# Weight sums between DRAM and DRAM, and a convolution tap added by an accumulating DMA, in a two-layer encoder kernel

## The chip, the core and the metric

The kernel runs on one core of a Trainium2 chip. The core has five engines that run side by side, each through its own queue of instructions: TensorE (PE: matrix products, with PEld loading its stationary operand), VectorE (DVE), ScalarE (ACT), GpSimd (POOL) and SyncE (SP, which here only issues transfers). Sixteen DMA engines move data for all of them. Tiles live in SBUF (128 partitions), products are collected in PSUM banks of 128 x 512 words. The metric is the device time of one execution in microseconds, the median of several; less is better.

## What is computed

Two layers, each a mixer of four branches followed by a convolutional FFN, over 512 tokens of 1024 channels, all in float32. The change touches the FFN's two later parts; of the mixer it matters that RMSNorm and the rotation of queries and keys come early in it. Cut to that:

```python
def _depthwise_conv(u, w, b):            # per channel, width 3, in the FFN
    y = lax.conv_general_dilated(u, w[:, None, :].astype(u.dtype), (1,), [(p, p)], ...)
    return y + b.astype(u.dtype)

def _conv_ffn(h, w_up, conv_w, conv_b, w_down):
    u = _depthwise_conv(h @ w_up, conv_w, conv_b)
    gate, up = jnp.split(u, 2, axis=-1)
    return (jax.nn.silu(gate) * up) @ w_down

def reference(...):
    for l in range(DEPTH):
        h = _rmsnorm(x, g_mix[l])
        proj = h @ w_in[l]
        ...
        cq = _partial_rope(_rmsnorm(cq, dil_qn[l]), cos, sin)
        ...
        x = x + mixed @ w_out[l]
        x = x + _conv_ffn(_rmsnorm(x, g_ffn[l]), w_up[l], ffn_conv_w[l], ffn_conv_b[l], w_down[l])
    return x
```

D_FF is 2816, so the FFN has 44 channel tiles of 128 (22 gates and 22 ups), and the down-projection contracts over 22 tiles, taken as 11 pairs.

## The kernel before

Every float32 product is three matmuls in a faster format: a weight is split into a high and a low part (`w_hi` by ACT, L222; `w_lo` by DVE, L224), an activation likewise, and high x high, low x high and high x low are summed in PSUM (`prod`, L243 to L245). Weights come in units of 128 x 1024 words, loaded by SP (L218) into `w_raw`. `unit` keeps two units ahead (`LOOK`), and three buffers hold splits. So a weight on its way to TensorE passes SP, ACT and DVE, in this order.

**Start of a layer.** `start_norm` and `norm_tile` make the scaled input and the sum of its squares. `finish_norm` turns that into 1/rms (`rstd`), which is needed along the tokens as a row for all partitions. It gets there through DRAM: POOL writes `row<-rstd` (L358) and reads it back as a broadcast, `raw<-row` (L362); ACT reorders it into `RB` (L366), which scales the products that leave PSUM. ACT's RB stands in front of the next `w_hi` splits. Then come the projections. For the dilated and the windowed branch, POOL rotates the first 16 channels of each head of Q in place (`qk_stats`, L510 to L513), and DVE scales Q after that (L519).

**Side work.** Attention, convolution and norms are generators in a list `side`. `tick` advances each by one step between blocks of TensorE's work, under `issue_after(self.last_mm.ins)`, which ties the instructions of a step that are TensorE's own behind the last matmul. What other engines get from a step is put in order by the scheduler: on each engine it takes what is ready by its own estimate of times, older work first.

**FFN** (`ffn`). A round i makes a gate tile and an up tile. Each is a block of 24 matmuls in one bank; DVE scales it into `U` (L915, with a zero column at either end); ACT writes the middle tap and the bias into `cy` (L918), and DVE adds the left and the right tap (L919, L920). ACT takes SiLU of the gate (`fth`, L924), DVE multiplies (`fl`, L931).

**Down-projection** (`down`). The contraction is a Winograd form of the product of 2 x 2 blocks, with seven products in place of eight. It needs sums of activations (`split_pair`, DVE) and sums of weights. A pair j of 128-row tiles has four weight quarters of 512 columns, b11, b12, b21 and b22; `weight_sums(l, j)`, called in every second round of the FFN, loads them into SBUF by POOL (`load_quad`, L971), forms t3, b12, t2 and b21 by four DVE subtractions (L978 to L981), and POOL stores the four to DRAM (L984). `last_units` lists the weight units of the down-projection, quarters from W and sums from that store; `w_raw<-sums` on SP reads them.

Of the kernel before, what the change touches and what calls it, by code (L numbers as in the profile page):

```python
# [31 lines left out]
NP2 = NF // 2  # L32

# [155 lines left out]
class Trunk:  # L189
# [484 lines left out]

    def attention(self, kind, V, yi):
# [214 lines left out]
    def ffn(self, l, last):  # L890
# [9 lines left out]
        self.load_quad(l, 0)  # L900
        for i in range(NF):
# [5 lines left out]
            if i % 2 == 0:  # L907

                with self.tc.issue_after(self.last_mm.ins):
                    self.weight_sums(l, i // 2)  # L910
            for s in range(2):
                c = i + s * NF
                ps = pss[s]
                u = U[(2 * i + s) % 4]
                v.tensor_tensor(u[:, 1:513], ps, self.RB, ALU.mult)  # L915
                y = self.fp.tile([P, S], F32, name=f"cy{s}", tag=f"cy{s}", bufs=2)
                w = lambda t: self.par('ffn_conv_w', c * 3 + t)
                nc.scalar.activation(y, u[:, 1:513], AF.Identity, scale=w(1), bias=self.par('ffn_conv_b', c))  # L918
                v.scalar_tensor_tensor(y, u[:, 0:512], w(0), y, ALU.mult, ALU.add)  # L919
# [35 lines left out]
    def last_units(self, l):  # L955

        quad = lambda j, q: self.quads[l][j][:, q * S:(q + 1) * S]
        sums = lambda j, a, b: self.sums[l][j][:, a * S:b * S]
        units = []
        for j in range(NP2):  # L960
            units.append(lambda j=j: [quad(j, 0), sums(j, 0, 1)])
            units.append(lambda j=j: [sums(j, 1, 3)])
        for f in (lambda j: quad(j, 2), lambda j: sums(j, 3, 4), lambda j: quad(j, 3)):
# [3 lines left out]
    def load_quad(self, l, j):  # L967

        self.quad = [self.fp.tile([P, 1024], F32, name="quad", tag="w_more", bufs=2) for _ in range(2)]
        for q in range(2):  # L970
            self.nc.gpsimd.dma_start(self.quad[q], self.quads[l][j][:, q * 1024:(q + 1) * 1024])  # L971

    def weight_sums(self, l, j):

        v = self.nc.vector
        (b11, b12), (b21, b22) = ((t[:, :S], t[:, S:]) for t in self.quad)
        t3, t2 = (self.fp.tile([P, S], F32, name=n, tag=n, bufs=1) for n in ("t3", "t2"))
        self.after_mm(v.tensor_tensor(t3, b22, b12, ALU.subtract))  # L978
# [3 lines left out]
        self.sums[l][j] = self.dram.tile([P, 4 * S], F32, name=f"sums{j}", tag=f"sums{j}", bufs=1)  # L982
        for n, t in enumerate((t2, b12, t3, b21)):
            self.nc.gpsimd.dma_start(self.sums[l][j][:, n * S:(n + 1) * S], t)  # L984
        if j + 1 < NP2:
            self.load_quad(l, j + 1)

    def pair_tags(self, j):
# [9 lines left out]
        s4 = (late[6:8], late[8:10], ["e6", "e7"], x[12:14], x[14:16], ["t3", "t2"])[j // 2]  # L998
        return hi + lo + a + s4

    def conv_tile(self, tag):
        w = {'U': 514, 'c': S}[tag[0]] + 4 * PHASE * (tag == 'U3')
        return self.fp.tile([P, w], F32, name=tag, tag=tag, bufs=1 if tag[0] == 'U' else 2)

    def split_pair(self, F, j, got):
# [5 lines left out]
        def tile(t):  # L1011
            pool = self.xpool if t[:2] in ("xh", "xl") else self.fp
            return pool.tile([P, S], F32R, name=f"p{t}", tag=t, bufs=2 if t in ("lo", "xr", "xn", "cy0", "cy1") else 1)
# [9 lines left out]
        def split(h, l, x):  # L1023
# [3 lines left out]
        v.tensor_tensor(a[:, lo], fi[:, hi], fk[:, hi], ALU.add)  # L1027
# [5 lines left out]
        v.tensor_tensor(fk[:, lo], fk[:, lo], a[:, hi], ALU.subtract)  # L1033
        split(bh, bl, fk[:, lo])
        cut = lambda h, l, c: [(h[:, c + b * P:c + (b + 1) * P], l[:, c + b * P:c + (b + 1) * P]) for b in range(2)]
        got[j] = {'a11': cut(ih, il, 0), 's3': cut(ih, il, 256), 'a12': cut(kh, kl, 0), 'a22': cut(kh, kl, 256),
                  's1': cut(ah, al, 0), 's2': cut(ah, al, 256), 's4': cut(bh, bl, 0)}

    def down(self, F, last):
# [24 lines left out]
        if last:  # L1064
            for b, h in ((2, 1), (3, 1), (0, 1), (1, 1), (2, 0), (3, 0), (0, 0), (1, 0)):
                nc.sync.dma_start(xt[b, h], self.resT[b * P:(b + 1) * P, h * S:(h + 1) * S])
            u = [self.fp.tile([P, S], F32, name="xn", tag="xn", bufs=2) for _ in range(2)]
        else:
            u = [xt[0, 1], xt[1, 1]]
# [8 lines left out]
        for b in range(2):  # L1078
            add(u[b], B[b])
        for b in range(2):  # L1080
            if last:
                add(xt[2 + b, 1], C[b])
            else:
                v.tensor_tensor(xt[2 + b, 1], u[b], C[b], ALU.add)
            add(xt[2 + b, 1], E[b])
        if last:
            for b in range(2):
                for t in (xt[2 + b, 1], xt[2 + b, 0], xt[b, 1]):
                    add(t, u[b])
                self.store(xt, 2 + b, 1)  # L1090
        for banks, x, n, h in ((A, 'a12', 0, 0), (E, 'a22', 2, 0), (C, 's4', 0, 1)):
# [11 lines left out]
            for b in range(2):  # L1103
# [7 lines left out]
                elif banks is E:  # L1111
                    v.tensor_tensor(t, u[b], banks[b], ALU.add)
# [26 lines left out]
    def run(self):  # L1139
        nc, tc = self.nc, self.tc  # L1140
        with ExitStack() as st:
# [8 lines left out]
            self.quads, self.sums = [], []  # L1150
            for l in range(L):
# [9 lines left out]
                self.sums.append([None] * NP2)  # L1161
# [48 lines left out]
    def layer(self, l):  # L1210
# [3 lines left out]
        with tc.tile_pool(name="gate", bufs=1, reuse_waits="tile") as self.gp:  # L1214
            with tc.tile_pool(name="attn", bufs=1, reuse_waits="tile") as self.ap:
# [5 lines left out]
                with self.first():  # L1221
                    for _ in self.qk_stats(Q, 4, 4, None):
# [5 lines left out]
                                 self.attention('na', V, 1)))  # L1228
                Vd = self.new_V()
# [37 lines left out]
        with tc.tile_pool(name="ffn", bufs=1, reuse_waits="tile") as self.fp:  # L1267
            self.scratch = lambda: self.fp.tile([P, S], F32, name="raw", tag="cy0", bufs=2)
# [59 lines left out]
```

## Time and profile before

| | |
|---|---|
| Median of 3 runs | 1559.25 us (1559.11 to 1559.95) |
| Span of the profiled execution, first to last instruction | 1556.7 us (the page gives no other time of it) |
| Mean granted clock of TensorE | 0.999 |
| First U of the FFN (L915) in layer 0, last `fl` (L931) in layer 1 | 452.42 us, 1456.30 us |
| First and last product of the down-projection | 673.01 us, 1552.05 us |
| DMA, whole span | 244.86 MB, 157 GB/s |

The profile is one execution, traced by the hardware. Its page gives the busy time of each engine, the span in 40 slices, the DMA queues, the chain of work that ended last (followed back from the end, at each step to what released it), and groups of instructions by line. The timeline and the waits are answers about a stretch or an engine. A time in brackets behind an instruction of the timeline is the idle time of its engine just before it and what ended it. Lines L1 and up are those of the kernel before, unless said otherwise.

### The profile page before, as it was taken

To read this page: it belongs to the slowest core of one execution; us is meant where nothing else is said; L and a number is where in the kernel's file an instruction comes from. 1 tells how busy PE (TensorE), PEld (TensorE's weight loads), DVE (VectorE), ACT (ScalarE), POOL (GpSimd) and SP (SyncE) were. 2 spreads that over 40 slices of the span, in tenths; PEclk is the share of its full clock that TensorE was granted. 3 is DMA by queue.
4 is the path that set the end of the run, shared out by engine and by line. 5 is a ranking of instruction groups with operands and counts; after the bars stand their busy time and mean duration, and the time that the engine had idled before them with its cause. 6 is when DMAs were issued, how large, how long until landed. Compare 5 with 4: busy or idle time off the path is not lost.

```text
span 1556.7 us, 20353 instructions
## 1 busy us (share of the span) xinstructions
PE 1550.7 (100%) x7122; PEld 1287.2 (83%) x7122; DVE 1235.9 (79%) x2102; ACT 834.7 (54%) x1420; POOL 174.8 (11%) x304
## 2 busy tenths in 40 slices
PE   9999999999999999999999999999999999999999
PEld 8888888888888888888888888888888888888887
DVE  6689988765689997796676899887656899977964
ACT  6778767333445443364457787672434444443643
POOL 0102002122001111100001020022120111111000
PEclk9999999999999999999999999999999999999999
DMA  7632222222645555576555422223226667655674
GB/s 236 192 93 87 83 81 82 95 98 93 215 162 203 192 187 187 202 238 211 188 181 184 117 72 87 74 76 108 95 95 211 194 221 238 202 203 191 219 231 165
DMA packets 103382, 244.86 MB, mean 157 GB/s; under 512 B 27504, under 2 KB 29424, under 8 KB 103280
## 3 DMA queue, kind: packets, MB, share of 16 engines
q1 hardware_dynamic: 89392, 196.37, 39.6%
q0 software_dynamic: 13600, 46.67, 8.5%
q8 instruction: 56, 0.92, 0.2%
q10 hardware_dynamic: 288, 0.52, 0.1%
q14 instruction: 46, 0.38, 0.1%
HBM read 202.63 MB, written 35.66 MB: 153 GB/s over the span
## 4 chain that ended last, share of the span: by engine, by line
PE 94%; DVE 3%; ACT 3%; issue 0%; ACTq 0%; DVEq 0%
PE mm L243 22%; PE mm L244 22%; PE mm L245 22%; PE aux L1048 3%; PE aux L1047 3%; PE aux L1046 3%; PE mm L467 2%; PE mm L469 2%; PE mm L468 2%; PE mm L1047 2%; PE mm L1048 2%; PE mm L1046 2%; PE aux L760 2%; PE aux L737 2%; PE aux L467 1%; PE aux L469 1%
## 5 line engine op out<-in xcount | busy, mean ns | idle before, releaser
L222 ACT ACTIVATE w_hi<-w_raw 128x1024 fp32r<-128x1024 f32 (+1 forms) x305 | 318.6, 1045 | 382.6 <-PE mm L244 218.9
L243 PE MATMUL mm<-xh,w_hi 128*128 128x512 f32 x1280 | 499.5, 390 | 0.0
L244 PE MATMUL mm<-xl,w_hi 128*128 128x512 f32 x1280 | 498.6, 390 | 0.0
L245 PE MATMUL mm<-xh,w_lo 128*128 128x512 f32 x1280 | 498.6, 390 | 0.0
L224 DVE TENSOR_TENSOR w_lo<-w_raw,w_hi 128x1024 fp32r<-128x1024 f32 (+1 forms) x305 | 368.7, 1210 | 83.4 <-ACT w_hi L222 81.3
L245 PEld LDWEIGHTS mm<-xh,w_lo 128*128 128x128 f32 x1280 | 240.3, 188 | 50.7
L243 PEld LDWEIGHTS mm<-xh,w_hi 128*128 128x128 f32 x1280 | 240.3, 188 | 49.1
L244 PEld LDWEIGHTS mm<-xl,w_hi 128*128 128x128 f32 x1280 | 240.3, 188 | 48.7
L836 POOL TENSOR_TENSOR mx<-mx,t 128x512 f32<-128x512 f32 x44 | 66.9, 1530 | 428.0 <-DVE t L835 327.1
L405 DVE SCALAR_TENSOR_TENSOR cv<-cv,prm 128x512 f32<-128x512 f32 x120 | 93.8, 781 | 0.7
L915 DVE TENSOR_TENSOR U<-mm,RB 128x512 f32<-128x512 f32 x88 | 60.0, 686 | 34.9 <-PE mm L245 34.8
L918 ACT ACTIVATE cy<-U,prm 128x512 f32<-128x512 f32 x88 | 70.7, 807 | 30.1 <-DVE U L915 29.9
L806 DVE TENSOR_TENSOR t<-mm,RB 128x512 f32<-128x512 f32 x64 | 43.9, 686 | 47.0 <-PE mm L245 46.8
L467 PE MATMUL mm<-w_hi,xh 128*128 128x512 f32 x192 | 76.4, 398 | 0.4 <-DVE V L595 0.4
L468 PE MATMUL mm<-w_lo,xh 128*128 128x512 f32 x192 | 75.0, 390 | 0.0
L469 PE MATMUL mm<-w_hi,xl 128*128 128x512 f32 x192 | 74.8, 390 | 0.0
L724 ACT ACTIVATE e<-e,rl 128x256 f32<-128x256 f32 (+2 forms) x96 | 57.3, 597 | 21.8 <-DVE rl L723 21.5
L920 DVE SCALAR_TENSOR_TENSOR cy<-U,prm,cy 128x512 f32<-128x512 f32 x88 | 65.5, 746 | 1.3
L919 DVE SCALAR_TENSOR_TENSOR cy<-U,prm,cy 128x512 f32<-128x512 f32 x88 | 65.3, 744 | 0.6 <-ACT cy L918 0.6
L924 ACT ACTIVATE fth<-cy 128x512 f32<-128x512 f32 x44 | 27.8, 632 | 64.1 <-DVE cy L920 64.0
L984 POOL DMA_DIRECT2D sums<-t x44 | 23.9, 544 | 339.4 <-DVE t L978 311.3
L717 ACT ACTIVATE e<-e,nm 128x256 f32<-128x256 f32 (+2 forms) x96 | 57.6, 600 | 2.7
(300 smaller groups left out, 2605.2 us busy)
## 6 DMA issues: line engine op xcount, KB each, us to landing
w_raw<-W SPq DMA_DIRECT2D x223, 512.0 KB, 3.5
quad<-W POOLq DMA_DIRECT2D x44, 512.0 KB, 5.3
w_raw<-W SPq DMA_DIRECT2D x66, 256.0 KB, 3.6
sums<-t POOLq DMA_DIRECT2D x44, 256.0 KB, 3.2
sums<-quad POOLq DMA_DIRECT2D x44, 256.0 KB, 3.8
w_raw<-sums SPq DMA_DIRECT2D x44, 256.0 KB, 3.8
w_raw<-sums SPq DMA_DIRECT2D x22, 512.0 KB, 4.4
res<-xn SPq DMA_DIRECT2D x24, 256.0 KB, 2.0
```

What stands on the lines that cost most here:

```text
L222: w = nc.scalar.activation(hi[:, s], raw[:, s], AF.Copy)
L224: nc.vector.tensor_tensor(lo[:, s], raw[:, s], hi[:, s].bitcast(F32), ALU.subtract)
L243: mm(ps, lhsT=wh, rhs=xh, start=start, stop=False)
L244: mm(ps, lhsT=wh, rhs=xl, start=False, stop=False)
L245: self.last_mm = mm(ps, lhsT=wl, rhs=xh, start=False, stop=stop)
L405: self.after_mm(v.scalar_tensor_tensor(acc, u[:, t:t + S], w(t), acc, ALU.mult, ALU.add))
L467: mm(pss[b], lhsT=self.Xh[k][:, t], rhs=hi[:, s], start=k == 0, stop=False)
L468: mm(pss[b], lhsT=self.Xh[k][:, t], rhs=lo[:, s], start=False, stop=False)
L469: self.last_mm = mm(pss[b], lhsT=self.Xl[k][:, t], rhs=hi[:, s], start=False, stop=k == KT - 1)
L1046: mm(ps, lhsT=x[0], rhs=w[0][:, cols], start=start, stop=False, skip_group_check=again)
L1047: mm(ps, lhsT=x[0], rhs=w[1][:, cols], start=False, stop=False, skip_group_check=again)
L1048: self.last_mm = mm(ps, lhsT=x[1], rhs=w[0][:, cols], start=False, stop=stop, skip_group_check=again)
```

## The change

Four things change together.

1. **Weight sums.** They are formed without SBUF or VectorE, by POOL's transfers between DRAM and DRAM: a copy of a quarter into the place of a sum, then a transfer that adds another quarter to it (`accum_op=ALU.add`). Eight steps a layer, each cut in three chunks (four, four and three pairs): 24 transfers of 512 or 384 rows of 2 KB. The generator `weight_sums(l)`, wrapped in `slowly`, is put into `side` once, at the start of the layer's mixer: it waits twelve ticks, and then issues one transfer every three.
2. **One tap.** ACT scales the left tap into a tile of its own (`cz`), DVE adds the right tap to that, and POOL adds `cz` to `cy` by an accumulating transfer in SBUF. `cy` gets three buffers, `cz` takes two of the tag `w_more`; `quad`, `t3` and `t2` are gone.
3. **Signs.** All sums of weights are now plain additions; the sums of activations change sign and role to match (`split_pair`).
4. **Order of the down-projection's last three products and of its output tiles**, as the new signs ask.

```diff
+    def slowly(self, g):
+        for _ in range(12):
+            yield
+        for _ in g:
+            for _ in range(SLOW):
+                yield
...
                 nc.scalar.activation(y, u[:, 1:513], AF.Identity, scale=w(1), bias=self.par('ffn_conv_b', c))
-                v.scalar_tensor_tensor(y, u[:, 0:512], w(0), y, ALU.mult, ALU.add)
-                v.scalar_tensor_tensor(y, u[:, 2:514], w(2), y, ALU.mult, ALU.add)
+                z = self.fp.tile([P, 1024], F32, name="cz", tag="w_more", bufs=2)[:, :S]
+                nc.scalar.activation(z, u[:, 0:512], AF.Copy, scale=w(0))
+                v.scalar_tensor_tensor(z, u[:, 2:514], w(2), z, ALU.mult, ALU.add)
+                nc.gpsimd.dma_start(y, z, accum_op=ALU.add)
...
-    def weight_sums(self, l, j):
-        v = self.nc.vector
-        (b11, b12), (b21, b22) = ((t[:, :S], t[:, S:]) for t in self.quad)
-        t3, t2 = (self.fp.tile([P, S], F32, name=n, tag=n, bufs=1) for n in ("t3", "t2"))
-        self.after_mm(v.tensor_tensor(t3, b22, b12, ALU.subtract))
-        v.tensor_tensor(b12, b12, b11, ALU.subtract)
-        v.tensor_tensor(t2, b22, b12, ALU.subtract)
-        v.tensor_tensor(b21, b21, t2, ALU.subtract)
...
+    def weight_sums(self, l):
...
+        for d, s in ((s3, b12), (s1, b11)):
+            for part, t, src in items:
+                add(part(t, d), part(src, s))
+                yield
+        for d, s in ((s3, b11), (s1, b21)):
+            for part, t, src in items:
+                add(part(t, d), part(src, s), accum_op=ALU.add)
+                yield
+        for d, b, s in ((s2, s3, b21), (s4, s2, b22)):
+            for part, t, src in items:
+                add(part(t, d), part(t, b))
+                yield
+            for part, t, src in items:
+                add(part(t, d), part(src, s), accum_op=ALU.add)
+                yield
...
                 self.queue(chain(self.na_biases(l, 3 if l else 5), self.qk_norm(Q, 4, 4, 0),
                                  self.attention('na', V, 1)))
+                self.side.append(self.slowly(self.weight_sums(l)))
```

Where the scheduler puts this can be read in the order of each engine's queue. POOL's queue at the start of the program, before: two rows of zeros for the convolution, the transfers of `finish_norm`, and the rotation of Q.

```order
L377 MEMSET cv_1091 128x15
L378 MEMSET cv_1091 128x15
L358 DMA row_337<-rstd_197 128x4 [waits DVE_49]
L362 DMA raw_339<-row_337 128x512 [waits DMAHW1_49,DMASW0_49,DMAHW2_49,PE_49,Activation_49]
L510 ISA
L510 TENSOR_TENSOR rA_928<-Q_625,rc0_389 128x64 [waits Activation_49]
```

POOL's queue now, from its first transfer (`sums0`, `sums4`, `sums8` are the chunks; those with numbers 773 to 775 belong to layer 0, 8036 to 8038 to layer 1; L995 and L1003 are copies, L999 and L1006 accumulations; DMASW names a transfer that POOL waits for):

```order
L995 DMA sums0_773<-W 512x512
L995 DMA sums4_774<-W 512x512
...
L999 DMA sums0_773<-W 512x512 [waits DMASW0_49]
...
L362 DMA row_337<-rstd_197 128x4 [waits DVE_49]
L1003 DMA sums4_8037<-sums4_8037 512x512 [waits DMASW7_49]
L1003 DMA sums8_8038<-sums8_8038 384x512 [waits DMASW0_49]
L1006 DMA sums0_8036<-W 512x512 [waits DMASW4_49]
L366 DMA raw_339<-row_337 128x512 [waits DMASW5_49,DMAHW1_49,DMASW1_49,DMAHW2_49,PE_49,Activation_49]
...
L1006 DMA sums8_8038<-W 384x512 [waits DMASW6_49,DMASW1_49]
L514 ISA
L514 TENSOR_TENSOR rA_934<-Q_625,rc0_389 128x64 [waits Activation_49]
```

Of the 48 transfers of both layers, 37 now stand ahead of `row`, 40 ahead of `raw` and all 48 ahead of the rotation. ACT's queue at RB is the same as before, row for row:

```order
L505 ACTIVATE sqq_359<-Q_344 128x512 [waits Activation_49]
L370 ACTIVATE RB_663<-raw_339 128x512 [waits DMASW1_49]
L226 ACTIVATE w_hi_547<-w_raw_546 128x1024 [waits DMAHW4_49,PE_49]
L226 ACTIVATE w_hi_634<-w_raw_633 128x1024 [waits DMAHW5_49,PE_49]
L547 ACTIVATE KH_518<-aux_520,qg_382 64x512 [waits PE_49]
```

Two splits of weights stand directly behind RB. The other place is the end of a round on DVE. Before, in round 7 of layer 0:

```order
L919 SCALAR_TENSOR_TENSOR cy1_5206<-U3_4472,prm_73,cy1_5206 128x512 [waits Activation_49]
L920 SCALAR_TENSOR_TENSOR cy1_5206<-U3_4472,prm_73,cy1_5206 128x512 [waits DVE_49]
L931 TENSOR_TENSOR fl7_5210<-cy1_5206,fth_5203 128x512 [waits DVE_49]
L1027 TENSOR_TENSOR sum_5740<-fl6_5115,fl7_5210 128x256 [waits DVE_49]
L1028 TENSOR_TENSOR fl6_5115<-fl6_5115 128x256 [waits DVE_49]
```

And now, in the same round:

```order
L928 SCALAR_TENSOR_TENSOR cz_5201<-U3_4499,prm_73,cz_5201 128x512 [waits DVE_49,Activation_49]
L922 TENSOR_TENSOR U0_4490<-mm_5207,RB_4544 128x512 [waits PE_49]
L940 TENSOR_TENSOR fl7_5205<-cy1_5199,fth_5196 128x512 [waits DMASW1_49]
L228 TENSOR_TENSOR w_lo_5290<-w_raw_5288,w_hi_5289 128x1024 [waits DMAHW5_49,Activation_49]
L928 SCALAR_TENSOR_TENSOR cz_5272<-U0_4490,prm_73,cz_5272 128x512 [waits DMASW0_49,DVE_49,Activation_49]
```

The product `fl` has moved behind the next round's first U, and waits for the accumulating transfer.

More of the change, by code (lines that the diff above doesn't have):

```diff
@@ L957, in last_units, with sums @@
         quad = lambda j, q: self.quads[l][j][:, q * S:(q + 1) * S]
-        sums = lambda j, a, b: self.sums[l][j][:, a * S:b * S]
+        def sums(j, a, b):
+            c = j // CHUNK
+            return self.sums[l][c][(j - c * CHUNK) * P:(j - c * CHUNK + 1) * P, a * S:b * S]
         units = []
         for j in range(NP2):
-            units.append(lambda j=j: [quad(j, 0), sums(j, 0, 1)])
+            units.append(lambda j=j: [quad(j, 1), sums(j, 0, 1)])
             units.append(lambda j=j: [sums(j, 1, 3)])
-        for f in (lambda j: quad(j, 2), lambda j: sums(j, 3, 4), lambda j: quad(j, 3)):
+        for f in (lambda j: quad(j, 3), lambda j: quad(j, 2), lambda j: sums(j, 3, 4)):
@@ L964, in last_units @@
             units.extend(lambda f=f, js=js: [f(j) for j in js] for js in PHASES)
         self.w_list.extend((0, u) for u in units)
[L967 to L971, printed above, removed]
-    def weight_sums(self, l, j):
-        v = self.nc.vector
-        (b11, b12), (b21, b22) = ((t[:, :S], t[:, S:]) for t in self.quad)
-        t3, t2 = (self.fp.tile([P, S], F32, name=n, tag=n, bufs=1) for n in ("t3", "t2"))
-        self.after_mm(v.tensor_tensor(t3, b22, b12, ALU.subtract))
-        v.tensor_tensor(b12, b12, b11, ALU.subtract)
-        v.tensor_tensor(t2, b22, b12, ALU.subtract)
-        v.tensor_tensor(b21, b21, t2, ALU.subtract)
[L982 to L986, printed above, removed]
+    def weight_sums(self, l):
+        add = self.nc.gpsimd.dma_start
+        items = []
+        for c in range(0, NP2, CHUNK):
+            n = min(CHUNK, NP2 - c)
+            t = self.dram.tile([n * P, 4 * S], F32, name=f"sums{c}", tag=f"sums{c}", bufs=2)
+            self.sums[l].append(t)
+            src = self.all_quads[l][c * P:(c + n) * P]
+            part = lambda x, i: x[:, i * S:(i + 1) * S]
+            items.append((part, t, src))
+        s2, s1, s3, s4 = range(4)
+        b11, b12, b21, b22 = range(4)
+        for d, s in ((s3, b12), (s1, b11)):
[13 more added lines that the diff above has]
+                yield
@@ L1079, in down, with less @@
             add(u[b], B[b])
+        def less(t, x):
+            v.tensor_tensor(t, t, x, ALU.subtract)
         for b in range(2):
+            t = xt[2 + b, 0]
             if last:
-                add(xt[2 + b, 1], C[b])
-            else:
-                v.tensor_tensor(xt[2 + b, 1], u[b], C[b], ALU.add)
-            add(xt[2 + b, 1], E[b])
+                less(t, C[b])
+                add(t, E[b])
+            else:
+                v.tensor_tensor(t, u[b], C[b], ALU.add)
+                v.tensor_tensor(t, E[b], t, ALU.subtract)
         if last:
             for b in range(2):
[L1088 to L1091, printed above, removed]
+                less(xt[2 + b, 0], u[b])
+                less(xt[b, 0], u[b])
+                add(xt[2 + b, 1], u[b])
+                self.store(xt, 2 + b, 0)
+        for banks, x, n, h in ((A, 'a12', 0, 1), (E, 'a22', 0, 0), (C, 's4', 2, 1)):
             whole = len(PHASES) - 2 * (banks is C)
@@ L1149, in run @@
             self.w_list = []
[L1150 removed]
+            self.quads, self.sums, self.all_quads = [], [], []
             for l in range(L):
```

33 lines of the change are left out of this document (16 added, 17 removed).

## The prediction

> **What bounds the kernel now.** I read the page first: busy time, slices, chain.
>
> ```profile
> span 1556.7 us, 20353 instructions
> PE 1550.7 (100%) x7122; PEld 1287.2 (83%) x7122; DVE 1235.9 (79%) x2102; ACT 834.7 (54%) x1420; POOL 174.8 (11%) x304
> ...
> PEclk9999999999999999999999999999999999999999
> DMA  7632222222645555576555422223226667655674
> ...
> PE 94%; DVE 3%; ACT 3%; issue 0%; ACTq 0%; DVEq 0%
> ```
>
> TensorE is busy 1550.7 of 1556.7 us at the full granted clock, and the chain that ended last lies on it for 94%. Only 6.0 us are idle, so no edit that leaves the matmuls alone can win more than 6 us (0.4%). The change leaves their number alone. What it can do is make TensorE wait, so I looked for what lies between POOL and TensorE. First the stretches (window, its length, then busy us and count of PE, PEld, DVE, ACT, POOL; clock, DMA share, GB/s):
>
> ```profile
> 0.00:39.00 39.00, 37.82 (x169) 31.77 (x170) 26.39 (x62) 23.73 (x36) 1.66 (x10) 1.00 0.73 236
> 39.00:78.00 39.00, 38.61 (x189) 31.88 (x188) 26.41 (x59) 27.37 (x57) 4.48 (x16) 1.00 0.64 191
> 78.00:117.00 39.00, 38.99 (x205) 32.74 (x204) 34.86 (x91) 29.27 (x73) 2.93 (x9) 1.00 0.31 94
> ...
> 507.00:546.00 39.00, 39.00 (x174) 32.30 (x173) 35.49 (x53) 17.39 (x24) 6.48 (x12) 1.00 0.60 201
> ```
>
> In the FFN (507 to 546) TensorE never idles, though VectorE is at 35.49 of 39 us: relieving VectorE there brings nothing by itself. A matmul takes 39/174 = 0.224 us, a weight unit of 24 of them 5.4 us. At the start the DMA engines are busiest (0.73).
>
> Then the timeline of POOL, ACT and DVE in the first layer:
>
> ```profile
> 32.27 0.68 POOL L358 DMA_DIRECT2D row<-rstd  x1 [31.30 <-DVE rstd L277]
> 35.48 0.55 POOL L362 DMA_DIRECT2D raw<-row  x1 [2.54 <-ACT Q L600]
> 73.20 0.32 POOL L510 TENSOR_TENSOR rA<-Q,rc 128x64 f32<-128x64 f32 x1 [37.17 <-ACT Q L600]
> ...
> 38.91 1.13 ACT L366 ACTIVATE RB<-raw 128x512 f32<-128x512 f32 x1 [1.33 <-DMA raw<-row]
> 39.93 1.05 ACT L222 ACTIVATE w_hi<-w_raw 128x1024 fp32r<-128x1024 f32 x1
> 44.87 1.06 ACT L222 ACTIVATE w_hi<-w_raw 128x1024 fp32r<-128x1024 f32 x1 [3.88 <-PE mm L469]
> ...
> 89.06 0.68 DVE L519 TENSOR_TENSOR Q<-Q,r_y 128x512 f32<-128x512 f32 x1
> ```
>
> POOL is on the way twice. At 35 us it issues the transfer `raw`, for which ACT waits at 38.91 (RB); queued behind RB on ACT are the w_hi splits, without which TensorE has no weights. At 73 us it starts the rotation of Q (L510), which DVE needs at 89.06. That POOL holds its queue for a transfer shows in the waits (engine, instruction, releaser: us in total, times, longest):
>
> ```profile
> POOL quad L971 <- DMA sums<-quad: 71.6, 40, 5.7
> ```
>
> **The change part by part.** *Weight sums.* Gone are 88 VectorE operations on whole tiles (L978 to L981) and 176 POOL transfers. In their place come 48 POOL transfers between DRAM and DRAM, 24 a layer. The generator that issues them is meant to pace them, but it holds back no transfer: by the order, six copies stand first on POOL, with no wait, ahead of `row` and `raw`, and 40 of the 48 (both layers' share) stand ahead of `raw`, all 48 ahead of the rotation. Each accumulating one waits on POOL for the copy into the same rows. So POOL reaches `raw` only when nearly all that traffic is done. That is the term that decides.
>
> One plane (512 columns of all eleven blocks) is 11 x 128 rows x 2 KB = 2.88 MB. Ahead of `raw` stand 7 planes of copies (four of layer 0, three of layer 1) and 6.36 planes of accumulation (four, and two and 4/11). No row shows DRAM to DRAM, nor an accumulating transfer. The nearest rows:
>
> ```profile
> q0 software_dynamic: 13600, 46.67, 8.5%
> ...
> q1 hardware_dynamic: 4032, 8.72, 59.9%
> q10 hardware_dynamic: 288, 0.52, 3.1%
> ...
> DMA packets 122, 0.19 MB, mean 189 GB/s; under 512 B 30, under 2 KB 30, under 8 KB 122
> ...
> q1 hardware_dynamic: 122, 0.19, 80.2%
> ...
> raw<-row POOLq DMA_DIRECT2D x1, 256.0 KB, 3.4
> ```
>
> The first is POOL's queue over the span (packets, MB, share of 16 engines): 46.67 MB in 0.085 x 1556.7 us is 353 GB/s for loads and stores, 8.2 us a plane. The q1 and q10 rows are the window 0 to 45 us: the start's own loads take (0.599 + 0.031) x 45 = 28 us of all engines. The 122 packets are the window 114 to 115 us, where little but KL<-KL and KH<-KH ran, copies within one memory: 189/0.802 = 236 GB/s, 12.2 us a plane. That is the row nearest to a copy within DRAM, and I take it. An accumulation reads two rows for each that it writes, a copy one; I take twice the copy, 24.4 us (an estimate from the same row). The bounds: as cheap as a plain load, 8.2 us, for both; or four copies, 48.8 us, for the accumulation.
>
> Data ahead of `raw`: 28 + 7 x 12.2 + 6.36 x 24.4 = 28 + 85 + 155 = 268 us; it lands 3.4 us later, at 272. ACT stands from its 38.9 on. TensorE still has what is split: the split at 44.87 waited for a buffer to come free, so it has one to two units in hand, 5 to 11 us; I take 8, it stops at the work of 47 us. After `raw` come RB 1.13, w_hi 1.05 and the DVE split 1.2, 3.4 us. The delay is 272 + 3.4 - 47 = **229 us**. The second wait agrees with it: the rotation needs 8 and 7 planes and 57 us of loads (0.73, 0.64 and 0.31 of the three stretches, the last to 89), 57 + 98 + 171 = 326; add 1.8 for one rotated block, less 89 and some 5 that TensorE has in hand, 233. By the bounds: 28 + 13.36 x 8.2 = 138, a delay of 98; and 28 + 85 + 310 = 423, 383 (403 by the rotation). Nothing hides this: all that TensorE does next needs splits. SP's loads of the sums, one stage later, find them done.
>
> The Trainium skill, "DMA: Bandwidth & Descriptors", section Latency and other measured facts, gives copies between HBM tensors 207 to 214 GB/s per direction. By it a plane costs 13.7 us and, with twice that for accumulation, the delay is 258 us (an estimate); the row of this trace is 236, and no run before shows which holds. "Collectives: The Full Stack", section The bandwidth ceiling, puts a reduce at half a copy's rate because the add needs "two source reads"; it speaks of rings between cores.
>
> *The tap.* Per channel tile one VectorE tap goes and one ACT scaling comes, with a transfer of 256 KB that adds z into y:
>
> ```profile
> L918 ACT ACTIVATE cy<-U,prm 128x512 f32<-128x512 f32 x88 | 70.7, 807 | 30.1 <-DVE U L915 29.9
> L919 DVE SCALAR_TENSOR_TENSOR cy<-U,prm,cy 128x512 f32<-128x512 f32 x88 | 65.3, 744 | 0.6 <-ACT cy L918 0.6
> ...
> L978 DVE TENSOR_TENSOR t<-quad x22: 677/683/686, 444.7 to 1435.4; 128x512 f32<-128x512 f32 x22
> ```
>
> A round of two tiles is two units, 10.9 us. VectorE loses per round 2 x 0.744 and two sums of 0.683: 9.9 (35.49/39 x 10.9) becomes 7.1. ACT gains 1.6 on 4.9. Queued behind the wait for the transfer are `fth` on ACT and `fl` on DVE, and behind them splits; `fl` now stands behind the next round's U. Since the splits are a unit ahead, only a sustained wait beyond 10.9 - 7.1 = 3.8 us a round costs TensorE. I take nothing; bounds -6.0 (all idle time won) and, with 6 us waited in each of 44 rounds, 44 x 2.2 = 97. *Signs, order, tiles and the tail:* the same matmuls, the same last add and store: nothing, within 1 us.
>
> **The sum.** 1556.7 + 229 = 1786 us of span. The page gives no other time of the profiled execution; the median of the runs, 1559.25, stands 2.5 above its span, so **1788 us**.
>
> **The rivals.** *Not slower:* the transfers do drain in time, or POOL does not hold `raw` behind them. It is decided at ACT's RB: 38.5 MB and the start's 9.2 would have to pass by 47 us, 1.0 TB/s against 353 in the row. For it: the change asks for pacing, and a paced stream over the attention (DMA share 0.31) would be free. Price: 1559 less what part of 6 us is won, plus nothing. Against: the order, and POOL's 40 waits for transfers. This is also the case that the change does what it says: 6%. *The FFN alone:* transfers quick enough at the start, but `fl` and `fth` wait: up to 97 us, 1563 to 1656; 4%. *Dearer still:* accumulation at six copies (73 us a plane) gives 28 + 85 + 466 = 579 and a delay of 535, 2095; or forecast and FFN waits together, from 1960 by the upper bound on: 12%. The forecast, ACT held at RB, has 78%.
>
> **How the numbers follow.** The range is the forecast's own: 1556.7 + 2.5 + 98 = 1657 and, with 403, 1962; I set 1650 to 1960, which leaves out some 20%. Slower by over 0.2% (what a measurement here can tell from no change): 78 + 12 + 4 = 94%; within 0.2%: 5%; faster: 1%, the two halves of the first rival.
>
> **What would show it.** In the profile of the changed kernel: a gap of some 230 us on TensorE near 47 us, ended on ACT by the transfer `raw`; POOL waiting for transfers of sums from its first microseconds; DMA share near 0.9 there; after it matmuls as dense as before, and no idle time in the FFN. Wrong would be: `raw` issued before 60 us; the gap at L519 alone; the first 24 transfers done in under 80 us; or TensorE idle in the FFN by more than 10 us.

## The result, and the profile after

| | before | after |
|---|---|---|
| Median of 4 runs each, side by side on one chip | 1559.32 us (1559.11 to 1559.95) | 1837.15 us (1836.43 to 1837.5) |
| Ratio, 95% interval | | 1.1782 [1.1765, 1.1798] |
| Span of the profiled execution | 1556.7 us | 1835.7 us |
| TensorE busy, idle | 1550.7, 6.0 us | 1608.7, 227.0 us |

The change costs 278 us; the forecast was 229. The sign, the mechanism at the start and the range hold. But that the total came near is luck in part, by two errors of opposite sign: of the 279 us that the span grew, the start costs 160, less than forecast, and the FFN 119, where I had put nothing.

The page of the changed kernel: span, busy time, TensorE's busy share and granted clock in 40 slices, the DMA share, and the chain that ended last.

```profile
span 1835.7 us, 20251 instructions
PE 1608.7 (88%) x7122; PEld 1314.8 (72%) x7122; DVE 1124.8 (61%) x1926; ACT 884.3 (48%) x1508; POOL 218.6 (12%) x308
...
PE   7600599999999999987799999999999999888699
...
PEclk9755799999999999999899999999999999999799
DMA  9999942223235544444666633223225566544565
...
PE 53%; issue 30%; DMA 8%; POOL 5%; DVE 2%; ACT 2%; POOLq 0%; SPq 0%; ACTq 0%; DVEq 0%
```

A slice is 46 us. The first five are the start: TensorE empties while the DMA engines are full, and the clock falls to half. The 8 and the two 7s from slice 18 on, and the 8s and the 6 near the end, are the two FFNs with their passages to the down-projection. The same 7122 matmuls are busy 58 us longer: part of the loss is no idle time at all, but for the most part matmuls at a lower clock (46 of the 58 us, see the last section).

Where the time went is read by counting matmuls. The n-th matmul of the changed kernel is set beside the n-th of the kernel before (start times in us, of all 7122 matmuls of each trace):

```
matmul   before    after    later by
   150     34.5     52.2      17.8
   300     66.8    222.0     155.2
   450     96.2    256.4     160.2
  2250    481.9    642.0     160.0    in the FFN of layer 0
  2400    515.9    677.8     161.9
  3000    651.9    837.8     185.8    its last rounds
  3150    685.9    900.7     214.8    in the down-projection
  5700   1230.2   1444.9     214.7    in the FFN of layer 1
  6600   1434.2   1687.8     253.6    its last rounds
  6750   1468.2   1747.2     279.0    in the down-projection
  7050   1536.2   1815.2     279.0
```

The delay grows at three places only: 160 us in the first 260 us, 55 in the first FFN and its passage to the down-projection, 64 in the second.

**The start.** The timeline of POOL, ACT and TensorE (start, duration, instruction; in brackets the idle time before it and its releaser), and the stretch 117 to 156 us of the windows (length, busy time and count of PE, PEld, DVE, ACT, POOL; clock, DMA share, GB/s):

```profile
1.27 3.90 POOL L995 DMA_DIRECT2D sums<-W  x6 [0.83 <-POOLq L1350]
...
161.78 0.59 POOL L362 DMA_DIRECT2D row<-rstd  x1
...
180.39 0.98 POOL L366 DMA_DIRECT2D raw<-row  x1
...
191.36 1.11 ACT L370 ACTIVATE RB<-raw 128x512 f32<-128x512 f32 x1 [127.57 <-DMA raw<-row]
...
193.45 2.36 DVE L228 TENSOR_TENSOR w_lo<-w_raw,w_hi 128x1024 fp32r<-128x1024 f32 x2 [123.69 <-ACT w_hi L226]
...
198.34 0.76 PE L471 MATMUL mm<-w_hi,xh 128*128 128x512 f32 x1 [118.88 <-DVE V L599]
...
214.19 0.94 POOL L1006 DMA_DIRECT2D sums<-W  x1 [2.25 <-DMA sums<-sums]
228.62 0.32 POOL L514 TENSOR_TENSOR rA<-Q,rc 128x64 f32<-128x64 f32 x1 [13.48 <-ACT Q L604]
...
117.00:156.00 39.00, 0.00 (x0) 0.00 (x0) 0.00 (x0) 0.00 (x0) 8.03 (x10) 0.50 1.08 217
```

Here the forecast's chain stands as written: POOL comes to `raw` at 180.39, after 40 of the sums' transfers; ACT stands before RB for 127.57 us; TensorE stands for 118.88. Its row names DVE's V as releaser, which is only the last link of the chain: DVE itself had stood for 123.69, for the split `w_hi` that stands behind RB on ACT. While they stand, nothing but the sums' transfers moves.

**The FFN.** The waits (engine, instruction, releaser: us in total, times, longest), and two stretches of the first FFN:

```profile
ACT fth L933 <- DMA cy<-cz: 209.3, 43, 10.2
DVE fl L940 <- DMA cy<-cz: 106.5, 40, 5.7
...
741.00:780.00 39.00, 34.78 (x142) 27.89 (x142) 21.91 (x31) 17.93 (x25) 6.05 (x7) 0.91 0.48 120
858.00:897.00 39.00, 22.64 (x72) 16.22 (x71) 22.26 (x35) 16.15 (x25) 3.44 (x4) 0.79 0.50 132
```

The window shown of before had 174 matmuls in 39 us; here 142 fit, and in the passage 72. All engines have idle time, and the DMA engines are half free: no engine is the bound, so it must be a chain of waits. The timeline of DVE, POOL, ACT and, in the last line, TensorE shows it over one round, about 742 us:

```profile
740.13 0.75 DVE L928 SCALAR_TENSOR_TENSOR cz<-U,prm,cz 128x512 f32<-128x512 f32 x1
741.17 0.88 POOL L929 DMA_DIRECT2D cy<-cz  x1 [4.26 <-DVE cz L928]
744.70 0.63 ACT L933 ACTIVATE fth<-cy 128x512 f32<-128x512 f32 x1 [5.84 <-DMA cy<-cz]
745.24 0.80 ACT L925 ACTIVATE cy<-U,prm 128x512 f32<-128x512 f32 x1
745.95 0.71 ACT L927 ACTIVATE cz<-U,prm 128x512 f32<-128x512 f32 x1
746.69 0.75 DVE L928 SCALAR_TENSOR_TENSOR cz<-U,prm,cz 128x512 f32<-128x512 f32 x1 [4.08 <-ACT cz L927]
747.74 0.87 POOL L929 DMA_DIRECT2D cy<-cz  x1 [5.68 <-DVE cz L928]
751.03 0.69 DVE L940 TENSOR_TENSOR fl<-cy,fth 128x512 f32<-128x512 f32 x1 [2.99 <-DMA cy<-cz]
751.64 1.22 DVE L228 TENSOR_TENSOR w_lo<-w_raw,w_hi 128x1024 fp32r<-128x1024 f32 x1
752.78 0.74 DVE L928 SCALAR_TENSOR_TENSOR cz<-U,prm,cz 128x512 f32<-128x512 f32 x1
753.97 0.86 POOL L929 DMA_DIRECT2D cy<-cz  x1 [5.36 <-DVE sum L1048]
...
752.92 0.80 PE L249 MATMUL mm<-xh,w_lo 128*128 128x512 f32 x1 [4.00 <-DVE w_lo L228]
```

Read it as a ring. The gate tile's transfer starts at 741.17; ACT's SiLU (`fth`) waits for it, and behind SiLU, in ACT's queue, stand the scalings of the up tile (`cy`, `cz`), for which DVE's second `cz` waits, for that the second transfer, for that DVE's `fl`, and behind `fl`, in DVE's queue, the next gate tile's `cz` (the last of POOL's rows names the sum behind that `cz` on DVE). One turn, from gate transfer to gate transfer, takes 753.97 - 741.17 = 12.8 us; TensorE's round takes 10.9. The count of matmuls agrees: from the 2400th to the 3000th, 12.5 rounds of 48, the delay grows by 24 us, 1.9 a round, which is 12.8 - 10.9. Nothing in the data asks for it: the two tiles are independent. The ring closes through the order of two queues, and splits of weights stand in both: in this round DVE's `w_lo` comes behind `fl`, and TensorE stands 4.00 us for it.

### The profile page after: what moved, and what is told of

It reads as the page before. It is cut to its first block, busy times and chain, and to the rows that moved or that the text cites. A ratio compares the mean times of both kernels' runs of the same rounds, so it can differ in the third digit from the quotient of the medians.

```text
span 1835.7 us, 20251 instructions
## 1 busy us (share of the span) xinstructions
PE 1608.7 (88%) x7122; PEld 1314.8 (72%) x7122; DVE 1124.8 (61%) x1926; ACT 884.3 (48%) x1508; POOL 218.6 (12%) x308
## 4 chain that ended last, share of the span: by engine, by line
PE 53%; issue 30%; DMA 8%; POOL 5%; DVE 2%; ACT 2%; POOLq 0%; SPq 0%; ACTq 0%; DVEq 0%
PE mm L247 11%; PE mm L248 11%; PE mm L249 11%; POOL cy L929 4%; PE aux L1067 2%; PE aux L1068 2%; PE aux L1069 2%; DMA sums<-W 2%; DMA sums<-sums 2%; PE mm L1067 1%; PE mm L1069 1%; PE mm L1068 1%; PE aux L772 1%; PE aux L749 1%; PE mm L471 1%
## 5 line engine op out<-in xcount | busy, mean ns | idle before, releaser
L249 PE MATMUL mm<-xh,w_lo 128*128 128x512 f32 x1280 | 510.1, 399 | 49.7 <-DVE w_lo L228 49.7
L247 PE MATMUL mm<-xh,w_hi 128*128 128x512 f32 x1280 | 507.2, 396 | 0.0
L248 PE MATMUL mm<-xl,w_hi 128*128 128x512 f32 x1280 | 506.0, 395 | 0.0
L249 PEld LDWEIGHTS mm<-xh,w_lo 128*128 128x128 f32 x1280 | 244.6, 191 | 113.2 <-DVE w_lo L228 61.4
L248 PEld LDWEIGHTS mm<-xl,w_hi 128*128 128x128 f32 x1280 | 244.9, 191 | 50.8
L247 PEld LDWEIGHTS mm<-xh,w_hi 128*128 128x128 f32 x1280 | 245.3, 192 | 49.9
L928 DVE SCALAR_TENSOR_TENSOR cz<-U,prm,cz 128x512 f32<-128x512 f32 x88 | 65.9, 749 | 154.8 <-ACT cz L927 154.7
L929 POOL DMA_DIRECT2D cy<-cz x88 | 76.0, 870 | 590.7 <-DVE cz L928 477.7
L471 PEld LDWEIGHTS mm<-w_hi,xh 128*128 128x128 f32 x192 | 38.0, 198 | 130.9 <-issue 121.2
L933 ACT ACTIVATE fth<-cy 128x512 f32<-128x512 f32 x44 | 27.8, 632 | 209.3 <-DMA cy<-cz 209.3
L940 DVE TENSOR_TENSOR fl<-cy,fth 128x512 f32<-128x512 f32 x44 | 30.5, 692 | 110.4 <-DMA cy<-cz 106.5
```

The costliest lines, as they stand in the source:

```text
L247: mm(ps, lhsT=wh, rhs=xh, start=start, stop=False)
L248: mm(ps, lhsT=wh, rhs=xl, start=False, stop=False)
L249: self.last_mm = mm(ps, lhsT=wl, rhs=xh, start=False, stop=stop)
L471: mm(pss[b], lhsT=self.Xh[k][:, t], rhs=hi[:, s], start=k == 0, stop=False)
L929: nc.gpsimd.dma_start(y, z, accum_op=ALU.add)
```

## The experiments

The theory after the result: (A) POOL's queue, blocked by accumulations that wait for their copies, costs the start, and the tap's ring costs the FFN, each by itself. Rivals: (B) the traffic of the sums costs time wherever it stands, and through all of it; (C) at the start it is not the queue but the sharing of the DMA engines. Eleven kernels were run (four or five times each, the three e2 twice):

| kernel | median us | ratio to before, 95% |
|---|---|---|
| after | 1837.15 | 1.1782 [1.1765, 1.1798] |
| e1_paced | 1677.69 | 1.0769 [1.0745, 1.0793] |
| e1_oldtap | 1715.25 | 1.1004 [1.0988, 1.102] |
| e1_both | 1566.33 | 1.0045 [1.003, 1.006] |
| e3_fth | 1588.68 | 1.0192 [1.0175, 1.0209] |
| e2_raw_sp | 1698.88 | 1.0897 [1.0876, 1.0919] |
| e2_raw_rope | 1613.04 | 1.0347 [1.0326, 1.0368] |
| e2_copies | 1672.02 | 1.0725 [1.0704, 1.0747] |
| e3_fth_fl | 1578.19 | 1.0125 [1.0108, 1.0142] |
| e4_last | 1566.75 | 1.0052 [1.0038, 1.0065] |
| e4_ffn | 1611.41 | 1.0346 [1.0325, 1.0366] |
| e4_all | 1656.83 | 1.0628 [1.0613, 1.0643] |

Runs of the kernel before, taken along on the chip of each group, had medians of 1558.74 (e1 and e3_fth), 1558.76 (e2 and e3_fth_fl) and 1558.91 us (e4).

**One part at a time.** e1_paced ties each of the sums' transfers, in the scheduler's order, behind the last matmul (`after_mm`, as the old `weight_sums` did for its first subtraction). e1_oldtap undoes the tap. e1_both does both.

```diff
-        add = self.nc.gpsimd.dma_start
+        add = lambda *a, **k: self.after_mm(self.nc.gpsimd.dma_start(*a, **k))
```

```diff
-                z = self.fp.tile([P, 1024], F32, name="cz", tag="w_more", bufs=2)[:, :S]
-                nc.scalar.activation(z, u[:, 0:512], AF.Copy, scale=w(0))
-                v.scalar_tensor_tensor(z, u[:, 2:514], w(2), z, ALU.mult, ALU.add)
-                nc.gpsimd.dma_start(y, z, accum_op=ALU.add)
+                v.scalar_tensor_tensor(y, u[:, 0:512], w(0), y, ALU.mult, ALU.add)
+                v.scalar_tensor_tensor(y, u[:, 2:514], w(2), y, ALU.mult, ALU.add)
```

> The sums' transfers are tied behind the last matmul in the scheduler's order, so on POOL they stand behind row and raw; the tap stays changed. Theory A (two separate losses: POOL's queue holds raw, 160 us by the traces' matmul times, and the two FFNs wait for the tap's transfers, 118 us): 1837 - 160 = 1677 us (1668 to 1690), ACT's wait for raw back to some 1 us, the FFN gaps as in the changed kernel. Theory B (the extra DMA traffic itself slows what the engines load, wherever it is put): 1720 us or more, with new TensorE gaps in the attention.

> The tap as before (two VectorE taps), the sums' transfers as in the change, unpaced. Theory A: 1559 + 160 = 1719 us (1710 to 1730), no TensorE gap in the FFN. Rival (the FFN's gaps are from the down-projection's loads of sums, or from VectorE's changed order, not from the tap): FFN gaps stay, 1790 us or more.

> Sums paced as in e1_paced, tap as before. Theory A: both losses gone, 1559 us within 0.3%, at best 2 us under before since TensorE was idle for 6 us only. Theory B (traffic of the sums, 46 MB in the attention): 1580 us or more.

Measured: 1677.69, 1715.25 and 1566.33. The two parts are separate losses: 1677.69 - 1558.74 = 119 us with the tap alone in place, 156.5 with the sums unpaced alone, and 275 together, of the 278. In e1_paced TensorE is as dense at the start as before, and the ring is there unchanged (`fth` waits 209.9 us in it, 209.3 in the changed kernel); in e1_oldtap the FFN has no gap, and ACT's RB waits as long as in the changed kernel:

```profile
188.99 1.11 ACT L370 ACTIVATE RB<-raw 128x512 f32<-128x512 f32 x1 [124.78 <-DMA raw<-row]
```

So the two parts are as A has them; whether the start's loss is the queue's hold (A) or the sharing (C), these three do not tell. e1_both missed its mark a little: 7.6 us over before, where within 0.3% (4.7 us) was expected. By the count of matmuls, 2.8 us of it arise between the 900th and the 1200th, and 4.2 at the same stage of layer 1 (4500 to 4800). There the paced transfers run beside the loads of weights, and a split waits for one (ACT, timeline of e1_both):

```profile
201.69 1.06 ACT L226 ACTIVATE w_hi<-w_raw 128x1024 fp32r<-128x1024 f32 x1 [6.04 <-DMA w_raw<-W]
```

So B is not nothing: some 7 us, with the transfers paced. Nothing is added behind the 4800th matmul, so the new signs and the new order of the down-projection, which stand in this kernel too, cost nothing that shows.

**What blocks the start.** In e2_raw_sp and e2_raw_rope the sums are unpaced, as in the change, and the tap is the old one. e2_raw_sp lets SP issue `row` and `raw`, so that RB no longer stands behind POOL. e2_raw_rope also gives the rotation to VectorE, so that nothing on the path is POOL's.

```diff
-            nc.gpsimd.dma_start(row.rearrange("(p b) -> p b", p=P), rstd)
+            nc.sync.dma_start(row.rearrange("(p b) -> p b", p=P), rstd)
...
-            nc.gpsimd.dma_start(raw, row.unsqueeze(0).broadcast_to([P, S]))
+            nc.sync.dma_start(raw, row.unsqueeze(0).broadcast_to([P, S]))
...
-        g = nc.gpsimd
+        g = nc.vector
```

> Tap as before, sums unpaced as in e1_oldtap (1715 us), but row and raw are issued by SP, so they no longer stand behind the sums on POOL. Theory H (POOL's queue holds what stands behind it): the next thing held is the rotation of Q, which POOL reaches when it has issued the last sums transfer, near 215 us; DVE needs it at 89 us of before, so a delay of 215 + 2 - 89 - 5 = 123 us and 1682 us, with ACT's wait for raw gone and the gap ended by DVE's Q. Theory C (the sums fill the DMA engines and everything is late by that): 1715 us unchanged, ACT still waits for raw until near 190 us.

> As e2_raw_sp, and the rotation of Q runs on VectorE too, so nothing that TensorE needs stands behind the sums on POOL; the sums' traffic is unchanged. Theory H: only the slower loads remain, 18 us by the 150th matmul in the changed kernel and somewhat more after: 1580 to 1620 us. Theory C: 1700 us or more.

Measured: 1698.88 and 1613.04. The first shows the second hold of the prediction: RB comes at 78 us, and TensorE stands later instead, until POOL has issued its last transfer and reaches the rotation (timeline of e2_raw_sp, ACT, POOL, DVE, PE):

```profile
78.32 1.11 ACT L370 ACTIVATE RB<-raw 128x512 f32<-128x512 f32 x1 [13.89 <-DMA raw<-row]
...
221.96 0.68 POOL L514 TENSOR_TENSOR rA<-Q,rc 128x64 f32<-128x64 f32 x1
...
224.15 0.69 DVE L523 TENSOR_TENSOR Q<-Q,r_y 128x512 f32<-128x512 f32 x1 [82.23 <-POOL Q L517]
...
232.41 0.58 PE L711 MATMUL aux<-KH,QS 128*128 128x256 f32 x1 [85.70 <-DVE pt L757]
```

DVE stands 82.23 us for the rotated Q, and what TensorE waits for stands behind that in DVE's queue. The expected 1682 was too low by 17: it had no term for loads that are slow beside the sums, and TensorE is 41 us late by its 300th matmul before it comes to stand. With both waits gone, 1613.04 remains, 54 us over before, nearly all of it gathered by the 450th matmul (51.7 us). That is C's share: the loads share the DMA engines with the sums, and ACT's splits wait for them four times as long as before (waits from 0 to 110 us, e2_raw_rope, then before):

```profile
ACT w_hi L226 <- DMA w_raw<-W: 30.9, 10, 9.4
...
ACT w_hi L222 <- DMA w_raw<-W: 7.6, 4, 5.1
```

A's share is the rest, 1715.25 - 1613.04 = 102 us. Both rivals were right in part: **with the queue's hold taken away, two thirds of the start's loss go, and the third that is the traffic stays.** The other order, the hold without the traffic, was not run. The rotation on VectorE may have a small part in that third: up to the 300th matmul both e2 kernels are 41 us late, but of the 11 us that e2_raw_rope adds by the 450th, one gap of 2.04 us ends on the rotation.

**What a plane costs.** e2_copies is e1_oldtap with plain copies in place of all accumulations: the sums are not formed, and the down-projection's result is another.

```diff
-                add(part(t, d), part(src, s), accum_op=ALU.add)
+                add(part(t, d), part(src, s))
```

> As e1_oldtap (1715 us), but each accumulating transfer of the sums is a plain copy; the sums are not formed. The prediction's price (an accumulation costs two copies, 24.4 us a plane): raw lands some 75 us earlier, 1640 us. The price that the changed kernel's trace suggests (an accumulation costs what a copy costs, (191 - 28) / 13.36 = 12.2 us a plane): 1715 us within 12.

Measured: 1672.02, between the two expectations. ACT's RB comes 188.99 - 147.70 = 41.3 us earlier than in e1_oldtap:

```profile
147.70 1.11 ACT L370 ACTIVATE RB<-raw 128x512 f32<-128x512 f32 x1 [80.75 <-DMA raw<-row]
```

Ahead of `raw` stand 6.36 planes of accumulation, so one costs 41.3/6.36 = 6.5 us more than a copy. The DMA view gives both prices more directly. First, e2_copies from 100 to 120 us, where nearly all that runs are its copies; then the changed kernel from 145 to 160 us, where accumulations run (packets, MB, rate; queue, packets, MB, share of the sixteen engines):

```profile
DMA packets 1579, 6.05 MB, mean 303 GB/s; under 512 B 102, under 2 KB 102, under 8 KB 1579
...
q0 software_dynamic: 1579, 6.05, 97.9%
...
DMA packets 1507, 2.99 MB, mean 199 GB/s; under 512 B 47, under 2 KB 47, under 8 KB 1507
...
q0 software_dynamic: 1507, 2.99, 111.9%
```

By these rates a plane of 2.88 MB is 9.5 us as a copy and 14.5 as an accumulation. The prediction had 12.2 and 24.4. The difference of 5.0 is less than the 6.5 above; where the other 1.5 comes from was not looked into. Nor do the runs show that the add itself makes the difference: in these windows a packet of a copy has 6.05 MB/1579 = 3.8 KB, one of an accumulation 2.99 MB/1507 = 2.0 KB, though both move the same rows of 2 KB. The larger packets may be why a copy is quicker; no run gives both the same packets. The Trainium skill, "DMA: Bandwidth & Descriptors", section Latency and other measured facts, has 207 to 214 GB/s per direction for copies between HBM tensors, measured on the queues of SP and ACT with tiles of 128 x 16 KiB; the 303 here, from POOL's queue, is above it. The Trainium skill, "Collectives: The Full Stack", section The bandwidth ceiling, halves the rate where an add reads two sources, in rings between cores; here it is 199/303 = 0.66.

**The ring.** e3_fth and e3_fth_fl have paced sums and the new tap. e3_fth puts `fth` on ACT behind the scalings of the up tile; e3_fth_fl also puts `fl` on DVE behind the next gate tile's `cz`. The second edit is of the same kind as the first:

```diff
-                nc.scalar.activation(z, u[:, 0:512], AF.Copy, scale=w(0))
+                za = nc.scalar.activation(z, u[:, 0:512], AF.Copy, scale=w(0))
...
-                if s == 0:
-                    si = self.fp.tile([P, S], F32, name="fth", tag="fth", bufs=2)
-                    nc.scalar.activation(si, y, AF.Silu)
-                    ys[0] = si
+            si = self.fp.tile([P, S], F32, name="fth", tag="fth", bufs=2)
+            self.behind(nc.scalar.activation(si, ys[0], AF.Silu), za)
+            ys[0] = si
```

> As e1_paced, and on ACT the SiLU (fth) of a round is put behind the scaling cz of the round's second tile, so that the up tile's work no longer stands behind the wait for the gate tile's transfer. Theory A1 (a loop: fl waits for transfer 2, the next round's cz stands behind fl, transfer 1, fth, the second cz behind fth, transfer 2: 11.8 us against a round of 10.9): one transfer leaves the loop, the FFN loss nearly goes, 1560 to 1575 us. Rival A2 (the transfers slow the engines by traffic in SBUF or on POOL, order aside): no gain, 1670 us or more.

> As e3_fth (1588.7 us), and on DVE the product fl of a round is put behind the next round's first cz, so the second transfer leaves the loop as well. Theory A1: the rounds have no gap left, as in e3_fth; of the 22 us that e3_fth stands above e1_both, which lie at the passage from the FFN to the down-projection, little goes, since the last fl waits for the last transfer as before: 1575 to 1592 us. Rival (a wait in every round still costs): 1566 us, that of e1_both.

Measured: 1588.68 and 1578.19. One instruction of a round, moved behind the up tile's scalings in ACT's queue, wins 1677.69 - 1588.68 = 89 us, though it still waits for its transfer, and TensorE's delay hardly grows in the rounds (0.4 us in the second FFN's). But e3_fth missed its 1560 to 1575 by 14 us: what is left arises at the passages from FFN to down-projection, 8.6 and 13.3 us, and there the transfer's latency has no next round to hide in. In e3_fth_fl the passages cost 6.6 and 7.0.

**The passage.** e4_last is e3_fth_fl with the old tap in the last two of the 22 rounds.

```diff
+                if i < NF - 2:
...
+                else:
+                    za = nc.scalar.activation(y, u[:, 1:513], AF.Identity, scale=w(1), bias=self.par('ffn_conv_b', c))
+                    v.scalar_tensor_tensor(y, u[:, 0:512], w(0), y, ALU.mult, ALU.add)
+                    zd = v.scalar_tensor_tensor(y, u[:, 2:514], w(2), y, ALU.mult, ALU.add)
```

> Kernel: paced sums; SiLU and fl put one step later; in the last two rounds of each FFN the old tap on VectorE, elsewhere the transfer. Theory (what is left of the tap's cost is the end of the FFN, where fl of the last rounds waits for its transfer and the first splits of the down-projection wait for fl): the 6.6 and 7.0 us at the two passages go, 1578 less 13 = 1565, within 4. Rival (the passages are late because the order of SiLU and fl was changed, or by the sums' traffic): stays between 1574 and 1582.

Measured: 1566.75, as the theory had it. Its delay is 3.0 us before the first FFN and 3.0 behind it, 7.4 before the second and 7.4 behind. The tap by transfer now costs nothing; the 7.8 us left are those of e1_both. It wins nothing either: TensorE was the bound.

**A place for the sums.** e4_ffn is e1_both with the sums' generator begun with the FFN, where the kernel before had its loads of quarters. e4_all is e4_last with the same edit.

```diff
-                self.side.append(self.slowly(self.weight_sums(l)))
...
+            self.side.append(self.weight_sums(l))
             F = self.ffn(l, last)
```

> Kernel: old tap; the sums paced, one transfer a tick, and begun with the FFN (as before the change) in place of the attention. Theory (the 7.6 us left with both parts mended are splits that wait for weights beside the sums' traffic in the attention, where loads have little lead; POOL has nothing else to do in the FFN): 1556 to 1561, no change from before. Rival (the traffic costs the same wherever it stands, or the down-projection's first units come too late): 1564 to 1575. Neither expects to beat the kernel before by more than 3 us, since its TensorE is idle for 6.

> Kernel: as e4_last, with the sums begun in the FFN, so that the tap's transfers and the sums' waiting accumulations share POOL's queue. Theory (an accumulation that waits for its copy holds POOL's queue, here ahead of the tap's transfers, for 5 to 15 us each and 12 times a layer; a round has 10.9): TensorE idle in the FFN again, 1590 to 1660. Rival (the queue's hold does not matter, since fl is a round late anyway): 1560 to 1570.

e4_ffn measured 1611.41, outside both expectations: it was the largest miss of the study, and it shows what the pacing really is. Timeline of e4_ffn, POOL and ACT; then a stretch of the windows of e4_ffn, the same stretch of the kernel before, and one of e1_both in the attention:

```profile
390.46 0.65 POOL L980 DMA_DIRECT2D sums<-W  x1
396.45 4.17 POOL L980 DMA_DIRECT2D sums<-W  x6
405.21 1.04 POOL L980 DMA_DIRECT2D sums<-W  x1 [4.59 <-DMA sums<-W]
...
430.38 1.06 ACT L226 ACTIVATE w_hi<-w_raw 128x1024 fp32r<-128x1024 f32 x1 [4.92 <-DMA w_raw<-W]
...
420.00:460.00 40.00, 26.67 (x94) 18.14 (x93) 18.56 (x25) 11.69 (x16) 4.89 (x6) 0.85 1.09 267
...
420.00:460.00 40.00, 40.00 (x178) 33.10 (x178) 31.35 (x46) 15.63 (x19) 3.26 (x6) 1.00 0.52 181
...
80.00:120.00 40.00, 39.96 (x209) 33.57 (x208) 36.01 (x91) 28.65 (x71) 9.23 (x16) 1.00 1.00 256
```

The transfers leave at 390 us, 60 us ahead of the FFN they were tied to, seven almost at once. The tie sets their place in POOL's queue, but no semaphore goes with it: the transfers wait for nothing on TensorE. In the attention of e1_both, work of POOL's that waits for other engines stands between some of them (a rotation, for which POOL waits 28.39 us, between the transfers at 102.57 and 138.36); here POOL's last product of the attention starts at 389.24, and behind it they run off. They then fill the DMA engines (1.09) under the output projection, whose loads come late (TensorE is 19.8 us later behind it); layer 1 loses 33.7, part of it within the FFN's rounds. Full engines alone are not the loss: in e1_both they are as full from 80 to 120 us (1.00), and TensorE is busy for 39.96 of 40 us. The two places differ in what the kernel itself loads there: before the change the DMA share is 0.36 in the attention's stretch and 0.52 in this one. So the likely reason why the sums cost little in the attention is that its own loads leave room, and not that they are spread; no run tells the two apart. The theory that only the attention lacks room is wrong: its 7.0 us did go (delay 0.6 us at the 1800th matmul, and 0.1 added at the 4800th), but 53.5 came in their place.

e4_all measured 1656.83, within what the queue's hold led me to expect. Here POOL does wait for something: the first seven transfers leave at 390 to 396 us as in e4_ffn, and then one of the tap's transfers stands in front of the other sums and holds them back to the FFN (timeline of POOL and a stretch of the windows, e4_all):

```profile
460.12 0.93 POOL L947 DMA_DIRECT2D cy<-cz  x1 [60.06 <-DVE cz L946]
...
460.00:500.00 40.00, 31.47 (x128) 25.06 (x127) 16.05 (x23) 15.72 (x22) 12.39 (x14) 0.87 1.07 217
```

The output projection is nearly spared (6.3 us), and the loss arises within the first rounds of the FFN, 39 us in layer 0 and 49 in layer 1, where the tap's transfers share POOL's queue with the sums and the DMA engines (1.07) as well. e4_ffn loses nothing in the FFN of layer 0, with the DMA engines as full (share 1.03 from 460 to 500 us, TensorE busy for 40.00 of 40), but only nine of its 24 transfers are left by then. So the run agrees with the hold and doesn't prove it apart from the traffic.

No version beat the kernel before.

## Why the prediction was right and wrong

- **The bound: right.** TensorE sets the time; taking 176 instructions from DVE (2102 to 1926, 111 us less busy time) won nothing measurable in any version.
- **The place at the start: right.** `raw` on POOL behind the sums (180 us, where 35 was before), RB on ACT, and the rotation as a second hold of nearly the same length, are all in the traces (e2_raw_sp, e2_raw_rope).
- **The size at the start: too dear.** 229 was forecast, 160 came. The mis-sized term is the price of a plane: 12.2 and 24.4 us taken, 9.5 and 14.5 measured. With these, 28 + 7 x 9.5 + 6.36 x 14.5 = 187 us of data ahead of `raw`; it landed by 191.4, forecast 272. The row I chose, KL<-KL and KH<-KH, was the wrong nearest: it is 1 us of another queue, and POOL's queue in the span (353 GB/s) was nearer for copies. Twice a copy for an accumulation was too dear as well, 14.5/9.5 = 1.5 came. The rest of the term, in steps: 81 us less by that; 3.6 more, as TensorE started 7.0 us after the landing and not 3.4; 4.7 less, as it ran to the work of 51.7 us and not 47; 13.5 more after the restart, while the sums still drained: 229 - 81 + 3.6 - 4.7 + 13.5 = 160.
- **That the sum held only the queue: incomplete, and hidden in the total.** It has no term for loads that the sums slow down, and without the hold these make nearly all of the 51.7 us that e2_raw_rope loses up to the 450th matmul. In the change it lies beside the hold, since the engines are full either way; when the hold goes, it stays. My remark that a paced stream over the attention would be free was off by 7 us.
- **The tap: wrong.** The step that failed is the one that puts the tap at nothing, since "only a sustained wait beyond 10.9 - 7.1 = 3.8 us a round costs TensorE"; it cost 119 us. It fails twice. The slack was reckoned for DVE alone; ACT, 4.9 + 1.6 = 6.5 us busy a round, has 4.4 and waits 209.3/43 = 4.9 for `fth` alone. And I took the two waits one by one, though `fth` and `fl` close a ring through the two queues, two transfers long: 12.8 us a turn in the round shown. The passages, 29 and 25 us of the 119, were in no term: the last rounds have no next round to hide in. My upper bound of 97 was also short of 119.
- **The signs named.** TensorE idle in the FFN by more than 10 us was to mean a wrong step; it idles 16 us in the passage from 858 to 897 us alone, and it marked the step above. The gap was to begin near 47 us and does near 79, as the work up to it is itself 27 us late; the DMA share, forecast near 0.9, is over 1.0.
- **The rivals.** "Not slower" falls by e1_oldtap: with the tap undone the time is still 1715. "Forecast and FFN waits together" is the mechanism that came. It shared a chance of 12% with the dearer accumulation, and I had put it above 1960 since the start's term was dearer; so the main forecast, at 78%, comes near in time with half of the mechanism.

## What to carry to other kernels

A place in an engine's queue is no pacing: in these runs a transfer that waits for nothing left as soon as the queue got to it (seven within 10 us in e4_ffn), and one that waits held all that stands behind it, on whichever engine that was waited for (`raw` from 35 to 180 us, and with it ACT and TensorE). When a fast operation in a loop is replaced by a transfer, follow the loop through every in-order queue until it closes, and compare the turn with the round (here 12.8 and 10.9 us); where it is longer, try moving the consumer behind the next independent producer, which won 89 us here without a faster transfer. Look at the last round by itself, as nothing stands behind it to hide the latency. And before bulk traffic is moved to another stage, compare what that stage loads itself.

## What the hardware showed that I had not expected

**An idle TensorE restarts slow.** The granted clock is 0.50 in the stretch without matmuls (117 to 156 us, shown above), and the first matmul after it takes 0.76 us, where a dense stretch has 0.39. In the FFN short gaps are enough: 741 to 780 us has 0.91, and there 174 - 142 = 32 matmuls of 0.224 us, 7.2 us, were lost, with only 39 - 34.78 = 4.2 us idle, nearly all of it the one gap of 4.00 us; the matmuls after it start 0.43 us apart. In the whole trace the clock is at half for 92 us of TensorE's busy time, which makes 46 us of the 58 that it is busy longer; the other 12 were not taken apart. The Trainium skill, "TensorE: Matmul & The Clock Gate", section What's actually happening, has half rate after an idle window and full rate after a busy one; the trace agrees, with 0.50 without matmuls and 1.00 in a dense stretch.

**Small transfers are slow to land while the DMA engines are full.** `raw`, 256 KB, took 3.4 us to land before and 10.9 behind the sums' traffic; the loads of 512 KB, 3.5 us by the page's median, took 10.7 in e4_ffn from 420 to 460 us:

```profile
raw<-row POOLq DMA_DIRECT2D x1, 256.0 KB, 10.9
...
w_raw<-W SPq DMA_DIRECT2D x6, 512.0 KB, 10.7
```

What stays open: in e4_all, how much is POOL's hold and how much the traffic; why e4_ffn loses 33.7 us in layer 1 and 19.8 in layer 0; and whether an accumulation is dearer than a copy by the add or by its smaller packets. None was taken apart further.
